# Attention of 512 queries at once, and elementwise work moved from GpSimd to VectorE, in a one-layer hybrid encoder block

## The chip, the cores and the metric

One core of one Trainium2 chip runs the whole kernel in one launch. The metric is device time in microseconds, the median of several runs. The engines are TensorE (PE: matrix products, with PEld for its weight loads), VectorE (DVE), ScalarE (ACT), GpSimd (POOL) and SyncE (SP, which here issues most DMAs; ScalarE issues those of the weights).

## The reference

2048 tokens of width 1024 go through one layer with two branches. All matrix products work in float32.

```
h    = rms_norm(x, norm_gain)
proj = h @ w_in                       # 7168 columns: q,k,v,gate of A; q,k,v,gate of R; two merge gates
A: 8 heads x 64. Each chunk of 64 frames attends to its own chunk and the 8 before it;
   score = q.k / 8 + bias by clipped distance; softmax; @ v;  times silu(gate);  @ w_out_attn
R: 8 heads, key 64, value 128. Rotary, then retention with decay by |distance|, chunk-causal,
   GroupNorm per head;  times silu(gate);  @ w_out_ret
out = rms_norm(x + (sigmoid(m_a) * A + sigmoid(m_r) * R) @ w_out, final_gain)
```

For blocks of 512 queries (four tiles of 128) the keys are cut into blocks of 128. Query tile t needs the five key blocks t to t+4, counted from 512 keys before the block: its own tile and the four before it. In the sequence's first block of queries only the blocks from number 4 on exist.

## The kernel before

**Float32 by halves.** Operands of the large products are split into a high part (a ScalarE copy, rounded) and a low part (source minus high part, on VectorE or GpSimd). A product of two is then three products: high by high, high by low, low by high. The probabilities of attention are split the same way (`pth`, `ptl`), and V's high and low halves lie side by side in one weight tile `va`, so that a product with `pth` and one with `ptl` suffice.

**Stages.** The token axis is handled in two halves (s = 0 and 1). In order of TensorE: projection p0, attention and retention of half 0, projection p1, attention and retention of half 1, branch outputs ba and br (the merge), output projection out. The gate projections g0 and g1 are the filler of attention and retention. Projections and out use Strassen's seven products per chunk (`Strassen`), with sums `t1` to `t4` of the weight blocks (`sum`) and low parts (`prepare`, `make`); a job's `lo_pool` names the products whose low part GpSimd makes.

**Order.** All dense products form one stream. `step()` puts out the next dense step (three matmuls a step in most jobs); `fill(n)` puts out n of them. `later(n, fn)` defers an operation by n steps, `put(n, dst, src)` a store by n steps. So every operation has its place in an order written by hand, and each engine keeps that order. `Sometimes` keeps it only while `strict[0]` is set; for the merge it is off, and a planner orders ScalarE, VectorE and GpSimd there, until `br1`'s third chunk sets it again ahead of out.

**Attention before.** A unit is (head h, block b of 512, half un of it): 256 queries, two tiles of 128 (a = 0, 1). `soft` multiplies a query tile with the keys of its window into the PSUM region `wide`; one step later VectorE adds the bias and finds the minimum (`least`, into a `pr` tile, `mn`), after two steps ScalarE takes the exponential and its sum, after four VectorE's reciprocal and GpSimd's multiplication normalize the tile. `weighted` then takes six key blocks of 128 in three groups of two: TensorE transposes the probabilities into `tp`, ScalarE evicts `pth`, a step later VectorE `ptl`, and `PV_LAG` = 3 steps after the transposition the products with V go into `po`. Each product has 256 columns, both query tiles, and where a tile does not see a key block, VectorE sets its 128 columns to zero. After the second unit of a block ScalarE and VectorE fold `po` into `oa`, and GpSimd multiplies it by the gate.

The unit loop puts `soft` of unit m (a = 0, two steps, a = 1, one step) ahead of the three groups of unit m-1 (one step each). For the first block of the sequence `weighted` has one group for un = 0 and two for un = 1. Attention tiles come from a ring of `E_ATT` = 12 buffers and `PR_BUFS` = 4 `pr` buffers.

**Merge and out.** `finish_yr` multiplies retention's output by gate, gain (VectorE) and reciprocal deviation (GpSimd, L1248) and splits it into resident operands `R`. `ep_br` (L1290, L1291) forms gate times product on VectorE and adds branch A's part `ta` on GpSimd; SP stores it. `fill_wo` and `place_wo` form and split the sums of `w_out`. The first chunk of out (c = 0) forms its four sums and two of its low parts on GpSimd.

Of the kernel before, what the change touches and what calls it, by code (L numbers as in the profile page):

```python
# [11 lines left out]
F32 = mybir.dt.float32  # L12
# [42 lines left out]
E_PROJ = 19  # L55
E_ATT = 12
E_RET = 22
E_MRG = 23
PR_BUFS = 4
ATT_FILLS = (1.0, 1.0)  # L60
# [13 lines left out]
def hybrid_kernel(  # L74
# [261 lines left out]
    class Strassen(Chunk):  # L336
# [15 lines left out]
        def lean(self):  # L352
            return self.job.name[0] == "p"

# [18 lines left out]
        def prepare(self, n):  # L373
            self.sums(n)
            for s in SUMS_OF:
                if s[0] == PRODUCTS[n][1]:
                    self.sum(*s)
            late = pool if n in self.job.lo_pool else dve
            self.make(n, self.b[PRODUCTS[n][1]], late)
# [907 lines left out]
    def ep_br(s):  # L1287
        def epilogue(c, i, j, ps, got):
            g, ta = got
            dve.scalar_tensor_tensor(g, g, 1.0, ps, ALU.add, ALU.mult)  # L1290
            pool.tensor_tensor(g, g, ta, ALU.add)  # L1291
            put(7, mxscr[2 * s + i][2 * c + j], g)

        return epilogue
# [3 lines left out]
    def fill_wo(k):  # L1298
# [8 lines left out]

        def place(m, t, eng):
            later(1, lambda: act.copy(R[m][0][:, k, :], t))
            later(3, lambda: eng.tensor_tensor(R[m][1][:, k, :], t, r32(R[m][0][:, k, :]), ALU.subtract))  # L1310

        def sums():
            dve.tensor_tensor(s3, a[1, 0], a[0, 0], ALU.subtract)
            place(0, a[0, 0], pool)
            dve.tensor_tensor(s2, s3, a[1, 1], ALU.add)

        def rest():
            pool.tensor_tensor(s4, a[0, 1], s2, ALU.subtract)
            place(1, a[0, 1], dve)
            pool.tensor_tensor(a[1, 0], a[1, 0], a[1, 1], ALU.add)  # L1320
            place(3, a[1, 0], dve)

# [88 lines left out]
    def attention(s, sbp, ps_wide):  # L1411
# [3 lines left out]
        kts, vts, qts, bts, uts, oas, prs = {}, {}, {}, {}, {}, {}, {}  # L1415
        units = [(h, b, un) for h in range(HEADS) for b in (2 * s, 2 * s + 1) for un in range(2)]

# [56 lines left out]

        def soft(h, b, un, a):

            t = 2 * un + a
            nm = f"{h}_{b}_{t}"
# [11 lines left out]
            for part in range(2):  # L1490
                for j0, j1 in parts:
# [3 lines left out]
                    )  # L1495
            pr = sbp.tile([P, WIN], F32, tag="pr", bufs=PR_BUFS, name=f"pr_{nm}")
            mn = small.tile([P, 1], F32, tag="mn", name=f"mn_{nm}")
            rsum = small.tile([P, 1], F32, tag="rsum", name=f"rsum_{nm}")
            bt = bts[h]

            def least():
                dve.tensor_tensor_reduce(
                    pr[:, 0:w], sp, bt[:, WIN - w:WIN], 1.0, 3.0e38, ALU.add, ALU.min, mn,
                )

            def exps():
                act.activation(pr[:, 0:w], pr[:, 0:w], AF.Exp, bias=mn, scale=-1.0, accum_out=rsum)

            def normed():
                dve.reciprocal(rsum, rsum)  # L1510
                pool.tensor_scalar(pr[:, 0:w], pr[:, 0:w], rsum, 1.0, ALU.mult, ALU.mult)
# [3 lines left out]
            later(4, normed)  # L1515
            return pr

        def weighted(h, b, un, pr2):

            nk = 6 if b > 0 else 2 * un + 2  # L1520
            lo = [0, 1] if b > 0 else [0, 0]
            hi = [nk - 1, nk]
            o = po[:, un * 256:(un + 1) * 256]
            for gr in range(nk // 2):
                js = [2 * gr + 1, 2 * gr] if gr in (0, nk // 2 - 1) else [2 * gr, 2 * gr + 1]
                tp = ACC(f"tp_{h}_{b}_{un}_{gr}")
                ok, none, parts = [], [], []
                for n, j in enumerate(js):
                    for a in range(2):
                        c = (2 * n + a) * P  # L1530
                        if lo[a] <= j < hi[a]:
                            pe.transpose(
                                tp[:, c:c + P], pr2[a][:, (j - lo[a]) * P:(j - lo[a] + 1) * P], ident
                            )
                            ok.append(c)
                        else:
                            none.append(c)
                c0, c1 = ok[0], ok[-1] + P
                assert c1 - c0 == len(ok) * P

                def part(which, gr=gr, tp=tp, none=none, parts=parts, c0=c0, c1=c1):
                    t = E(f"pt{which}_{h}_{b}_{un}_{gr}", F32R)
                    parts.append(t)
                    for c in none:
                        dve.memset(r32(t[:, c:c + P]), 0.0)
                    if which == "h":
                        act.copy(t[:, c0:c1], tp[:, c0:c1])
                    else:
                        dve.tensor_tensor(t[:, c0:c1], tp[:, c0:c1], r32(parts[0][:, c0:c1]), ALU.subtract)

                def product(gr=gr, js=js, parts=parts):
                    for n, j in enumerate(js):
                        k = 2 * un + j if b > 0 else j + 4
                        v4 = vts[h, b - 1 + k // 4][:, k % 4, :]
                        for i, t in enumerate(parts):
                            pe.matmul(
                                o, v4, t[:, 256 * n:256 * n + 256],
                                start=(gr == 0 and n == 0 and i == 0),
                                stop=(gr == nk // 2 - 1 and n == 1 and i == 1),
                            )  # L1560
                    if gr == nk // 2 - 1:
                        later(1, out_)

                part("h")
                later(1, lambda part=part: part("l"))
                later(PV_LAG, product)
                yield

            def out_():
                if un == 0:  # L1570
                    return
                oa, u = E(f"oa_{h}_{b}")[0:64], uts[h, b]
# [3 lines left out]
                put(6, oascr[h // 2][b][64 * (h % 2):64 * (h % 2) + 64], oa)  # L1576

        load_bias(0)
        load_k(0, 2 * s)
        load_q(0, 2 * s, 0)  # L1580
        fill(12)
        turn_bias(0)
        fill(6)
        for m in range(len(units) + 1):
            if m < len(units):
                h, b, un = units[m]
                if m + 1 < len(units):
                    h2, b2, un2 = units[m + 1]
                    load_q(h2, b2, un2)
                if un == 0 and m + 2 < len(units):  # L1590
                    load_k(*units[m + 2][0:2])
                if un:
                    load_u(h, b)
                if (b, un) == (2 * s, 0) and h + 1 < HEADS:
                    load_bias(h + 1)
                if (b, un) == (2 * s + 1, 0) and h + 1 < HEADS:
                    turn_bias(h + 1)
                prs[m] = [soft(h, b, un, 0)]
                fill(2 * ATT_FILL)
                prs[m].append(soft(h, b, un, 1))  # L1600
                fill(ATT_FILL)
            if m:
                for _ in weighted(*units[m - 1], prs.pop(m - 1)):
                    fill(ATT_FILL)
            if m < len(units) and un == 0:
                later(PV_LAG - 1, lambda h=h, b=b: load_vs(h, b))
        fill(PV_LAG + 9)

# [431 lines left out]
```

## Time and profile before

| | us |
|---|---|
| median of 3 runs (1924.24 to 1926.1) | 1926.05 |
| the profiled execution | 1926.96 |
| its span, first to last instruction | 1925.2 |
| PE busy | 1879.2 |
| DVE busy | 1355.6 |
| ACT busy | 930.3 |
| POOL busy | 771.7 |

In the profiled execution attention takes 345 to 560 us (half 0) and 1060 to 1321 us (half 1) of the span, ba starts at 1491, br at 1583, out at 1758. In a row `out<-in xcount | busy, mean ns | idle`, the first names are program tiles without their numbers, the busy time counts overlapping matmuls once, and the last part is what the engine waited for just before. L143 is the line of a helper that records nearly every operation, so tiles, not lines, tell operations apart there.

### The profile page before, as it was taken

How to read it: one execution, taken by the hardware profiler on the slowest of the kernel's cores; microseconds unless marked ns; L12 is line 12 of the kernel's file. 1: busy time of each engine (PE TensorE's matmuls, PEld its weight loads, DVE VectorE, ACT ScalarE, POOL GpSimd, SP SyncE). 2: the span in 40 equal slices, each digit the busy share in tenths (PEclk: the TensorE clock that was granted, in tenths of full speed). 3: DMA queues.
4: the chain of work that ended last, by engine and by line, in shares of the span. 5: the costliest groups of instructions: out<-in, count | busy, mean ns of one | idle time of the engine just before them, and what ended most of it. 6: DMA issues, size and time to landing. Idle time of an engine off the chain costs nothing. (4 is left out here: it accounts for less than half of the span.)

```text
span 1925.2 us, 31831 instructions
## 1 busy us (share of the span) xinstructions
PE 1879.2 (98%) x10437; PEld 1617.7 (84%) x10437; DVE 1355.6 (70%) x2602; ACT 930.3 (48%) x1931; POOL 771.7 (40%) x661
## 2 busy tenths in 40 slices
PE   7999999999999999999999999999999999999998
PEld 6899889888888878899889888888888878887886
DVE  6879888677756558879797777765555654557665
ACT  7555553666655445443333656664455321223554
POOL 0102105545546562002105444544564114547775
PEclk9999999999999999999999999999999999999999
DMA  6586876665559987675666555555998999987673
GB/s 197 160 282 195 274 259 218 184 186 178 174 155 281 273 241 268 224 249 180 224 237 216 156 165 175 161 157 162 271 290 263 326 356 328 319 264 234 209 234 133
DMA packets 325555, 435.91 MB, mean 226 GB/s; under 512 B 29880, under 2 KB 191184, under 8 KB 325392
## 3 DMA queue, kind: packets, MB, share of 16 engines
q1 hardware_dynamic: 260096, 368.35, 59.9%
q10 hardware_dynamic: 65296, 65.55, 11.1%
q8 instruction: 83, 1.36, 0.3%
q14 instruction: 80, 0.66, 0.1%
HBM read 288.14 MB, written 145.64 MB: 225 GB/s over the span
## 5 line engine op out<-in xcount | busy, mean ns | idle before, releaser
L143 POOL TENSOR_SCALAR pr<-pr,rsum 128x640 f32<-128x640 f32 (+4 forms) x128 | 96.0, 750 | 213.3 <-DVE ptl L143 103.4
L143 PE MATMUL ps_g_x<-r,wh_g 128*128 128x512 f32 x448 | 143.9, 402 | 1.0 <-ACT u_g L143 0.8
L143 PE MATMUL ps_g_z<-r,wh_g 128*128 128x512 f32 x448 | 143.6, 402 | 0.7 <-DVE c_g L143 0.7
L143 DVE CUSTOM_DVE_ANT_0 pr<-wide,bt 128x640 f32<-128x640 f32 (+4 forms) x128 | 94.3, 736 | 62.5 <-PE wide L143 56.2
L143 ACT ACTIVATE pr<-pr,mn 128x640 f32<-128x640 f32 (+4 forms) x128 | 98.0, 766 | 81.1 <-DVE mn L143 81.1
L143 POOL TENSOR_TENSOR l_vr<-vrt,h_vr 128x512 fp32r<-128x512 f32 x32 | 47.7, 1492 | 202.3 <-DMA qrs<-l_q 131.5
L143 DVE TENSOR_TENSOR ptl<-tp,pth 128x384 fp32r<-128x384 f32 x168 | 96.0, 572 | 41.8 <-ACT pth L143 37.6
L143 ACT CAST pth<-tp 128x384 fp32r<-128x384 f32 x168 | 84.6, 515 | 69.0 <-PE tp L143 65.3
L143 POOL TENSOR_TENSOR sl<-sm,sh 128x384 fp32r<-128x384 f32 x64 | 69.9, 1092 | 70.2 <-ACT sh L143 44.7
L143 DVE TENSOR_TENSOR sm<-sr,dm 128x384 f32<-128x384 f32 x64 | 35.6, 556 | 83.6 <-PE sr L143 31.5
L143 PEld LDWEIGHTS tp<-ident,pr 128*128 128x128 f32 x560 | 71.2, 140 | 27.4 <-POOL pr L143 2.8
L143 PE MATMUL po<-pth,va 128*128 128x256 f32 x336 | 92.4, 295 | 0.9 <-DMA va<-vas 0.9
L143 ACT CAST wh_p<-raw_p 128x512 fp32r<-128x512 f32 x111 | 68.0, 619 | 50.3 <-PE ps_p_y L143 17.9
L143 PE MATMUL tp<-ident,pr 128*128 128x128 f32 x560 | 89.1, 272 | 3.0 <-POOL pr L143 1.9
L143 PE MATMUL wide<-ka,qa 128*128 128x384 f32 (+1 forms) x448 | 88.2, 313 | 2.2 <-DVE mn L143 2.1
L143 POOL TENSOR_TENSOR wl_g<-t_g,wh_g 128x512 fp32r<-128x512 f32 x56 | 74.8, 1336 | 38.4 <-ACT wh_g L143 31.0
L143 PEld LDWEIGHTS wide<-ka,qa 128*128 128x128 f32 x448 | 74.5, 188 | 18.6 <-DVE mn L143 8.7
L143 PE MATMUL po<-ptl,va 128*128 128x256 f32 x336 | 88.3, 284 | 1.4 <-DVE ptl L143 0.2
L143 PE MATMUL ps_g_x<-r,wl_g 128*128 128x512 f32 x224 | 88.5, 395 | 0.0
L143 POOL TENSOR_TENSOR yr<-yr,rb 128x512 f32<-128x512 f32 x8 | 11.7, 1467 | 191.1 <-DVE yr L143 100.1
L143 PE MATMUL ps_g_z<-r,wl_g 128*128 128x512 f32 x224 | 88.1, 393 | 0.0
L143 POOL TENSOR_TENSOR t_g<-raw_g,t_g 128x512 f32<-128x512 f32 x56 | 73.8, 1318 | 28.7 <-DVE wl_g L143 10.6
(929 smaller groups left out, 6193.3 us busy)
## 6 DMA issues: line engine op xcount, KB each, us to landing
raw_g<-in_w_in_dram ACTq DMA_DIRECT2D x56, 512.0 KB, 5.0
raw_p<-in_w_in_dram ACTq DMA_DIRECT2D x50, 512.0 KB, 6.3
qa<-qas SPq DMA_DIRECT2D x128, 128.0 KB, 3.3
qr<-qrs SPq DMA_DIRECT2D x128, 128.0 KB, 4.9
vr<-vrs SPq DMA_DIRECT2D x64, 256.0 KB, 5.8
ka<-kas SPq DMA_DIRECT2D x56, 256.0 KB, 3.7
va<-vas SPq DMA_DIRECT2D x40, 256.0 KB, 3.5
kds<-kdt_k SPq DMA_DIRECT2D x32, 256.0 KB, 5.5
```

The costliest lines, as they stand in the source:

```text
L143: return tc.keep_in_program_order(op(*a, **k))
```

## The change

Attention handles a whole block of 512 queries as a unit (h, b). `soft` takes one query tile t = 0 to 3, `weighted` one group of key blocks: (0, 1), (2), (3), (4), (5), (7, 6); the first block of the sequence uses the last three groups. Each product has only the columns of the query tiles that see the key block. `plan` gives a unit's length in slots of one dense step, which group stands in which slot and which query tile of the next unit stands in which; `slot` puts them out, with the loads. In the first block the four query tiles share two `pr` buffers. `E_ATT` goes from 12 to 11, `PR_BUFS` from 4 to 5, and the first group of a unit is multiplied after 4 steps, not 3.

Besides, these operations go from GpSimd to VectorE: the four sums and two low parts of out's first chunk, the multiplication by the reciprocal deviation in the merge (`m` given), the sum in `ep_br`, and sums and low parts in `fill_wo` and `place_wo`.

```diff
-E_ATT = 12
+E_ATT = 11
-PR_BUFS = 4
+PR_BUFS = 5
...
         def lean(self):
-            return self.job.name[0] == "p"
+            return self.job.name[0] == "p" or self.job.name == "out" and self.c == 0
...
-            late = pool if n in self.job.lo_pool else dve
+            late = pool if n in self.job.lo_pool and not self.lean() else dve
...
-        later(lead + 2, lambda: pool.tensor_tensor(a, a, r, ALU.mult))
+        later(lead + 2, lambda: (pool if m is None else dve).tensor_tensor(a, a, r, ALU.mult))
...
-            pool.tensor_tensor(g, g, ta, ALU.add)
+            dve.tensor_tensor(g, g, ta, ALU.add)
...
-            place(0, a[0, 0], pool)
+            place(0, a[0, 0])
...
-            pool.tensor_tensor(s4, a[0, 1], s2, ALU.subtract)
+            dve.tensor_tensor(s4, a[0, 1], s2, ALU.subtract)
...
-            pool.tensor_tensor(a[1, 0], a[1, 0], a[1, 1], ALU.add)
+            dve.tensor_tensor(a[1, 0], a[1, 0], a[1, 1], ALU.add)
...
-                eng = pool if k == 2 else dve
-                eng.tensor_tensor(R[m][1][:, k, :], wo[m, k], r32(R[m][0][:, k, :]), ALU.subtract)
+                dve.tensor_tensor(R[m][1][:, k, :], wo[m, k], r32(R[m][0][:, k, :]), ALU.subtract)
...
-        def soft(h, b, un, a):
-            t = 2 * un + a
+        def soft(h, b, t):
+            un, a = divmod(t, 2)
...
             def least():
+                pair, at = (t, 0) if b > 0 else ((0, 0), (1, 0), (1, 2 * P), (0, P))[t]
+                if (h, b, pair) not in wholes:
+                    wholes[h, b, pair] = sbp.tile([P, WIN], F32, tag="pr", bufs=PR_BUFS, name=f"pr_{nm}")
+                prs[h, b, t] = wholes[h, b, pair][:, at:at + w]
...
+        def weighted(h, b, gr):
+            k0 = 0 if b > 0 else 4
+            js = ((0, 1), (2,), (3,), (4,), (5,), (7, 6))[gr]
+            tp = ACC(f"tp_{h}_{b}_{gr}")
+            c, cut, parts = 0, [], []
+            for j in js:
+                ts = range(max(0, j - 4), min(4, j + 1))
+                cut.append((j, c, ts))
+                for t in ts:
+                    at = (j - max(t, k0)) * P
+                    pe.transpose(tp[:, c:c + P], prs[h, b, t][:, at:at + P], ident)
+                    c += P
...
+            def product():
+                for j, at, ts in cut:
+                    n = len(ts) * P
+                    v4 = vts[h, b - 1 + j // 4][:, j % 4, :]
+                    for i, p in enumerate(parts):
+                        pe.matmul(
+                            po[:, ts[0] * P:ts[0] * P + n], v4, p[:, at:at + n],
+                            start=j == (0 if b > 0 else 4) and i == 0, stop=gr == 5 and j == 6 and i == 1,
+                            skip_group_check=True,
+                        )
+                if gr == 5:
+                    later(1, out_)
...
+            part("h")
+            later(1, lambda: part("l"))
+            later(PV_LAG + (gr == 0), product)
+
+        def plan(b):
+            if b == 0:
+                return 9, {2: 3, 4: 4, 6: 5}, {1: 0, 3: 1, 5: 2, 7: 3}
+            return 12, {0: 0, 2: 1, 4: 2, 6: 3, 8: 4, 10: 5}, {2: 0, 6: 1, 8: 2, 10: 3} if s else {2: 0, 4: 3, 6: 1, 8: 2}
+
+        def slot(m, n, groups, softs):
+            after = units[m + 1] if m + 1 < len(units) else None
+            if n == 0 and after:
+                h, b = after
+                load_q(h, b, 1)
...
+            if n == 6:
+                if m + 2 < len(units):
+                    load_k(*units[m + 2])
+                if m >= 0:
+                    load_u(*units[m])
+            if n in groups and m >= 0:
+                weighted(*units[m], groups[n])
+            if n in softs and after:
+                soft(*after, softs[n])
...
-        fill(6)
-        for m in range(len(units) + 1):
...
-        fill(PV_LAG + 9)
+        fill(2)
+        for m in range(-1, len(units)):
+            length, *plans = plan(units[m][1] if m >= 0 else 2 * s + 1)
+            for n in range(length):
+                slot(m, n, *plans)
+                if n == length - 2 and m + 2 < len(units):
+                    load_q(*units[m + 2], 0)
+                if n == length - 1 and m + 1 < len(units):
+                    load_vs(*units[m + 1])
+                fill(ATT_FILL if m >= 0 or n > 1 else 0)
+        fill(PV_LAG + 3)
```

More of the change, by code (lines that the diff above doesn't have):

```diff
@@ L1306, in fill_wo, with place @@
         wo[4, k], wo[5, k], wo[2, k], wo[6, k] = s2, s3, a[1, 1], s4
-        def place(m, t, eng):
+        def place(m, t):
             later(1, lambda: act.copy(R[m][0][:, k, :], t))
-            later(3, lambda: eng.tensor_tensor(R[m][1][:, k, :], t, r32(R[m][0][:, k, :]), ALU.subtract))
+            later(3, lambda: dve.tensor_tensor(R[m][1][:, k, :], t, r32(R[m][0][:, k, :]), ALU.subtract))
         def sums():
             dve.tensor_tensor(s3, a[1, 0], a[0, 0], ALU.subtract)
-            place(0, a[0, 0], pool)
+            place(0, a[0, 0])
             dve.tensor_tensor(s2, s3, a[1, 1], ALU.add)
         def rest():
-            pool.tensor_tensor(s4, a[0, 1], s2, ALU.subtract)
-            place(1, a[0, 1], dve)
-            pool.tensor_tensor(a[1, 0], a[1, 0], a[1, 1], ALU.add)
-            place(3, a[1, 0], dve)
+            dve.tensor_tensor(s4, a[0, 1], s2, ALU.subtract)
+            place(1, a[0, 1])
+            dve.tensor_tensor(a[1, 0], a[1, 0], a[1, 1], ALU.add)
+            place(3, a[1, 0])
         later(10, sums)
@@ L1415, in attention @@
         kts, vts, qts, bts, uts, oas, prs = {}, {}, {}, {}, {}, {}, {}
-        units = [(h, b, un) for h in range(HEADS) for b in (2 * s, 2 * s + 1) for un in range(2)]
+        units = [(h, b) for h in range(HEADS) for b in (2 * s, 2 * s + 1)]
+        wholes = {}
         def load_k(h, b):
@@ L1495, in soft @@
                     )
-            pr = sbp.tile([P, WIN], F32, tag="pr", bufs=PR_BUFS, name=f"pr_{nm}")
             mn = small.tile([P, 1], F32, tag="mn", name=f"mn_{nm}")
@@ L1501, in least @@
             def least():
+                pair, at = (t, 0) if b > 0 else ((0, 0), (1, 0), (1, 2 * P), (0, P))[t]
+                if (h, b, pair) not in wholes:
+                    wholes[h, b, pair] = sbp.tile([P, WIN], F32, tag="pr", bufs=PR_BUFS, name=f"pr_{nm}")
+                prs[h, b, t] = wholes[h, b, pair][:, at:at + w]
                 dve.tensor_tensor_reduce(
-                    pr[:, 0:w], sp, bt[:, WIN - w:WIN], 1.0, 3.0e38, ALU.add, ALU.min, mn,
+                    prs[h, b, t], sp, bt[:, WIN - w:WIN], 1.0, 3.0e38, ALU.add, ALU.min, mn,
                 )
             def exps():
+                pr = prs[h, b, t]
                 act.activation(pr[:, 0:w], pr[:, 0:w], AF.Exp, bias=mn, scale=-1.0, accum_out=rsum)
             def normed():
+                pr = prs[h, b, t]
                 dve.reciprocal(rsum, rsum)
@@ L1515, in soft @@
             later(4, normed)
[L1516 to L1567, printed above, removed]
@@ new lines, in weighted, with part @@
+        def weighted(h, b, gr):
[10 more added lines that the diff above has]
+                    c += P
+            def part(which):
+                p = E(f"pt{which}_{h}_{b}_{gr}", F32R)
+                parts.append(p)
+                if which == "h":
+                    act.copy(p[:, 0:c], tp[:, 0:c])
+                else:
+                    dve.tensor_tensor(p[:, 0:c], tp[:, 0:c], r32(parts[0][:, 0:c]), ALU.subtract)
+            def product():
[10 more added lines that the diff above has]
+                    later(1, out_)
@@ L1569, in out_ @@
             def out_():
-                if un == 0:
-                    return
                 oa, u = E(f"oa_{h}_{b}")[0:64], uts[h, b]
@@ L1576, in out_ @@
                 put(6, oascr[h // 2][b][64 * (h % 2):64 * (h % 2) + 64], oa)
+            part("h")
[10 more added lines that the diff above has]
+                load_q(h, b, 1)
+                if b == 2 * s and h + 1 < HEADS:
+                    load_bias(h + 1)
+                if b == 2 * s + 1 and h + 1 < HEADS:
+                    turn_bias(h + 1)
+            if n == 6:
[7 more added lines that the diff above has]
+                soft(*after, softs[n])
@@ L1578, in attention @@
         load_bias(0)
-        load_k(0, 2 * s)
-        load_q(0, 2 * s, 0)
+        load_k(*units[0])
+        load_q(*units[0], 0)
         fill(12)
         turn_bias(0)
-        fill(6)
-        for m in range(len(units) + 1):
[L1585 to L1606, printed above, removed]
```

## The prediction

> **What bounds the kernel now.** I read the page's totals first, then busy time by stage, then TensorE's groups with shapes kept apart, its instructions in order of time, and its waits.
>
> The page's head and the row of PE:
>
> ```profile
> span 1925.2 us, 31831 instructions
> PE 1879.2 (98%) x10437; PEld 1617.7 (84%) x10437; DVE 1355.6 (70%) x2602; ACT 930.3 (48%) x1931; POOL 771.7 (40%) x661
> ```
>
> TensorE is busy 98% of the span, so the time follows what it is given to do plus its few waits. The two attention stages, by stretches (length, then busy time of PE, PEld, DVE, ACT and POOL, clock, DMA share, GB/s):
>
> ```profile
> 345.00:560.00 215.00, 211.91 (x1233) 180.12 (x1232) 157.08 (x456) 135.14 (x316) 117.40 (x132) 1.00 0.58 173
> 1060.00:1321.00 261.00, 256.58 (x1540) 221.91 (x1539) 189.26 (x520) 157.61 (x343) 126.44 (x128) 1.00 0.53 159
> ```
>
> PE idles 3.1 us in the first and 4.4 us in the second, at full clock; no other engine is over 73%. A busy PE hides cost, since matmuls overlap: a matmul's price is the distance from its start to the next start. PE in order of time (start, duration, operation, shape, count):
>
> ```profile
> 420.16 0.40 PE L143 MATMUL ps_g_v<-r,wl_g 128*128 128x512 f32 x1
> 420.39 0.33 PE L143 MATMUL wide<-ka,qa 128*128 128x128 f32 x2
> 420.56 0.33 PE L143 MATMUL po<-pth,va 128*128 128x256 f32 x1
> ...
> 421.78 0.28 PE L143 MATMUL po<-pth,va 128*128 128x256 f32 x1
> ...
> 422.25 0.63 PE L143 MATMUL ps_g_v<-r,wh_g 128*128 128x512 f32 x2
> ...
> 427.55 0.51 PE L143 MATMUL wide<-ka,qa 128*128 128x384 f32 x2
> 427.90 0.28 PE L143 MATMUL po<-pth,va 128*128 128x256 f32 x1
> ```
>
> The prices: 512 columns 0.23 us (420.16 to 420.39); two of 128 columns together 0.17, so 0.085 each; 256 columns 0.1175 (four `po` from 421.78 to 422.25); 384 columns 0.175 (two from 427.55 to 427.90).
>
> **The change, part 1: the products with V.** The groups before:
>
> ```profile
> L143 PE MATMUL po<-pth,va 128*128 128x256 f32 x336 | 92.4, 295 | 0.9 <-DMA va<-vas 0.9
> L143 PE MATMUL po<-ptl,va 128*128 128x256 f32 x336 | 88.3, 284 | 1.4 <-DVE ptl L143 0.2
> ```
>
> 672 products of 256 columns, 672 x 0.1175 = 79.0 us. After it each key block of 128 multiplies only the query blocks that see it. A full block of 512 queries (24 of them: 8 heads x 3) has key blocks that serve 1, 2, 3, 4, 4, 3, 2, 1 query tiles; each is multiplied twice (high and low part), which is 4 products each of 128, 256, 384 and 512 columns. A first block (8 heads) has only its own four key blocks, serving 4, 3, 2, 1: 2 of each width. Together 24 x 4 + 8 x 2 = 112 of each width: 112 x (0.085 + 0.1175 + 0.175 + 0.23) = 68.0 us. The saving is 11.0 us, all on PE, nothing beside it.
>
> The transposes stay 560, in 168 groups of three or four, so the evictions into `pth` and `ptl` stay; the score matmuls stay 448. The memsets of missing blocks go from VectorE. The dense steps interleaved are the same: 18 + 96 + 72 + 12 = 198 in the first attention stage before, 24 + 168 + 6 = 198 after; 222 and 222 in the second. So the work beside attention does not move.
>
> TensorE's waits in the two attention stretches, and who of PEld waited for the transposes' parts:
>
> ```profile
> PE tp L143 <- POOL pr L143: 0.9, 2, 0.8
> PE po L143 <- DMA va<-vas: 0.9, 1, 0.9
> PE wide L143 <- DVE mn L143: 0.8, 1, 0.8
> ```
>
> ```profile
> PE wide L143 <- DVE mn L143: 1.3, 1, 1.3
> PE tp L143 <- DVE ptl L143: 1.1, 2, 0.6
> PE tp L143 <- POOL pr L143: 1.0, 1, 1.0
> ```
>
> ```profile
>   PEld po L143: 4.2, 14
> ```
>
> **Late low parts.** 14 times the weight load of a `po` product waited for `ptl`, 4.2 us in all. They fall on a unit's first group. VectorE is in order there: in the rows below `oa` runs at 1133.64 and ends at 1134.30, and the next unit's first `po` product starts at 1134.43, its low part still behind `oa` on VectorE. After the change a unit's first group is multiplied one step later (lag 4, not 3), and its memsets are gone. I take -3.0, between 0 and -4.2. Next late is the `po` bank itself, below.
>
> **The softmax chain gets a step less.** One tile's way, with the reuse of `po`, in order of time over all engines:
>
> ```profile
> 1127.84 0.74 PE L143 MATMUL wide<-ka,qa 128*128 128x384 f32 x4
> ...
> 1128.62 0.82 DVE L143 CUSTOM_DVE_ANT_0 pr<-wide,bt 128x640 f32<-128x640 f32 x1 [0.22 <-PE wide L143]
> ...
> 1133.57 0.15 DVE L143 RECIPROCAL rsum<-rsum 128x1 f32<-128x1 f32 x1
> 1133.64 0.66 DVE L143 TENSOR_TENSOR oa<-po,oa 64x512 f32<-64x512 f32 x1
> ...
> 1133.89 0.80 POOL L143 TENSOR_SCALAR pr<-pr,rsum 128x640 f32<-128x640 f32 x1 [3.80 <-DVE rsum L143]
> ...
> 1134.43 0.36 PE L143 MATMUL po<-pth,va 128*128 128x256 f32 x1
> ```
>
> From the scores at 1127.84 to the normalized tile at 1134.69 it is 6.85 us. Before, the second tile of a unit has 7 steps until its first transposition, 7 x 261/222 = 8.2 us in the second stage. After, query tiles 1, 2 and 3 have 6: tile 2 goes from slot 8 to slot 2 of the next unit, tile 3 from 10 to 4. 6 steps at that mean are 7.1 us: 0.2 us of slack. VectorE's and GpSimd's own operations in it are only 0.82 + 0.15 + 0.80 = 1.8 us, most of the rest is queueing, so it can shrink; but GpSimd's sums for the gates stand in front of some. 64 uses (two a unit) are exposed. Bounds: 0, and 64 x 0.80 = 51 us if each waited for one more GpSimd operation of that size. Three waits of this kind cost 1.9 us at the old slack; I take +2.5, near the old rows, because slots that carry tiles are longer than the mean.
>
> **The output bank.** From a block's last product to the next block's first are four steps, and the read-out `oa` ends 0.13 us ahead of the latter (1134.30 and 1134.43). In the second stage the change leaves three steps, but VectorE's read is then queued ahead of the next tile's minimum instead of behind one. 0 to 15 blocks x 0.6 us = 9; I take +1.
>
> SP issues Q's parts 4 to 8 slots ahead, the ring of attention buffers shrinks from 12 to 11, and the one DMA wait is 0.9 us; zero, with the DMA wait in PE's list as its sign. The two `wide` waits at the stages' starts I leave as they are (the second half of Q is asked for two steps earlier or later).
>
> **Part 2: from GpSimd to VectorE.** GpSimd's largest group in the merge (29 under this line, three more under another), then, from the start of the output projection, VectorE alone and beside GpSimd, TensorE's long wait, and the stretch around it:
>
> ```profile
> L1291 POOL TENSOR_TENSOR gr<-gr,ta 128x512 f32<-128x512 f32 x29 | 44.5, 1540 | 56.9 <-DVE gr L1290 33.5 <-issue 16.1 <-DMA yr<-ors 3.3
> ```
>
> ```profile
> 1765.07 0.68 DVE L143 TENSOR_TENSOR wl_out<-raw_out,wh_out 128x512 fp32r<-128x512 f32 x1
> 1765.67 1.75 DVE L143 TENSOR_TENSOR r<-wo,r 128x512 fp32r<-128x512 f32 x1
> ```
>
> ```profile
> 1766.53 0.73 PE L143 MATMUL ps_out_x<-r,wh_out 128*128 128x512 f32 x2 [2.73 <-ACT u_out L143]
> ```
>
> ```profile
> 1754.00:1780.00 26.00, 22.93 (x92) 17.77 (x90) 24.61 (x21) 11.38 (x22) 23.71 (x15) 0.93 0.75 252
> ```
>
> Moved are 32 adds of the merge, 24 multiplications of `yr`, 12 of `fill_wo`, 4 of `place_wo`, and 6 of the first output chunk: 78, at 0.68 us 53 us for VectorE instead of 1.54 us each on GpSimd. They lie beside a full PE everywhere except at 1754 to 1780, where VectorE (24.6 of 26 us) and GpSimd (23.7) are both full and slow each other: 1.75 us against 0.68 for the same shape. There PE waits 2.73 us and then runs at clock 0.93, 0.07 x 26 = 1.8 us more. After: 21 + 13 operations at 0.68 = 23.1 us of VectorE, so it stays full, but each link is shorter. SP's stores of the merged rows wait for VectorE, done sooner, and no queue is passed. ScalarE, which makes `u_out`, also waited for a DMA, which stays. Bounds: -4.5 (both go) and +4.5 (a second such wait, should VectorE's longer queue hold ScalarE). I take -2.5.
>
> By the Trainium skill, TensorE: Matmul & The Clock Gate, section "What's actually happening", the array drops to half clock after an idle window of about 3.4 us. The row shows the clock at 0.93 behind an idle of 2.73 us, so the measurement decides. By the page this stall would have no clock price, and the term would be 1.8 us smaller: 1914.9 instead of the sum below.
>
> **Sum**: -11.0 - 3.0 + 2.5 + 1.0 - 2.5 = -13.0 us. The profiled execution took 1926.96 us (span 1925.2), 0.9 over the median of 1926.05; 1926.96 - 13.0 = 1913.96, and against the median 1913.1.
>
> **Rivals.**
> - *Narrow products pay a full weight load.* Each product loads its weights anew, and in retention, with three of 128 columns in a row, the later ones are 0.11 us apart:
>
> ```profile
> 604.33 0.28 PE L143 MATMUL o<-sl,vr 128*128 128x128 f32 x1
> 604.44 0.27 PE L143 MATMUL o<-sh,vr 128*128 128x128 f32 x1
> ```
>
> Then 112 x 0.025 = 2.8 us are lost: 1915.9. Against it: the pairs here follow a wide matmul, as at 420.39. The Trainium skill, same page, section "LDWEIGHTS (loading the stationary operand)", gives columns / 1.2 ns, an estimate of 107 ns for 128; by that rule the saving would be 8.5 us. The 0.17 us pair speaks against the rule for the first of two.
> - *The bank's reuse eats half*: 15 blocks x 0.6 us = 9 instead of 1: 1921.1. For it: `oa` ends 0.13 us before the next product now. Against: what delays it, the minimum in front, is behind it after.
> - *All stalls go*: -11.0 - 4.2 - 4.5 and no new waits: 1906.4, or lower with the starts.
> - *No change to measure*: the exposed tiles wait 0.24 us each (64 x 0.24 = 15.5, the other terms' -15.5): 1926.
> - *Slower*: transposes starve. At 0.24 us a use it turns; at 0.5 us it is 32 us against 15.5, 1942. For it: 0.2 us of slack and GpSimd 55% busy in the first stage. Against: 1.9 us of such waits now, and most of the 6.85 us is pacing by the steps.
>
> **How the numbers follow.** What a measurement can tell here is about 0.2%, 3.9 us. Forecast 0.53, narrow products 0.16, bank 0.12, all stalls gone 0.07, no change 0.05, slower 0.07. The first four are faster: 0.88; same 0.05; slower 0.07. The range 1906 to 1922 reaches over the first three (0.81) and leaves out 0.19.
>
> **What would show it.** `po` by shape: 224 each for `pth` and `ptl`, 112 each of 128, 256, 384 and 512 columns in all, and the two attention stretches about 5 us shorter each. "PEld po" behind `ptl` near 1 us. Waits of `tp` for `pr` under 5 us; over 15 I am wrong. DVE's operations of the merge near 0.7 us, and the 2.73 us wait shorter, the clock there 1.00. A wait of `po` for `oa`, or of `wide` for DMA `qa`, over 3 us would be the bank or the SP queue.

## The result and the profile after

| us | before | after |
|---|---|---|
| median of 5 runs each, on one chip | 1924.24 | 1909.69 |
| lowest to highest | 1921.62 to 1926.1 | 1905.84 to 1913.15 |
| the profiled execution | 1926.96 | 1909.69 |

The ratio is 0.9927, interval 0.9907 to 0.9946: 14.55 us faster. Forecast were 1913.1, in a range of 1906 to 1922, and a drop of 12.95. The two profiled executions are 17.3 us apart, since the one of before lies 2.7 us over its median here; terms read from the traces add up to that figure. The interval of the ratio leaves room for a drop of 10.4 to 17.9 us.

The head of the changed kernel's page, and its row of engines:

```profile
span 1907.9 us, 31062 instructions
...
PE 1866.9 (98%) x10213; PEld 1604.4 (84%) x10213; DVE 1355.7 (71%) x2456; ACT 933.1 (49%) x1931; POOL 665.3 (35%) x583
```

TensorE is as full as before in a shorter span: work went from the engine that bounds the kernel. GpSimd lost 106 us of busy time. VectorE's stayed, though 78 operations came: with the memsets gone it has 146 instructions fewer. The stretches that answer to those shown of before (the two attention stages, then 4 us ahead of out's first matmul to 22 us behind it; columns: length, busy PE, PEld, DVE, ACT, POOL, clock, DMA share, GB/s):

```profile
341.00:558.00 217.00, 213.68 (x1162) 180.01 (x1161) 150.90 (x362) 139.38 (x324) 120.11 (x135) 1.00 0.58 172
1052.00:1313.00 261.00, 258.39 (x1445) 220.25 (x1444) 179.11 (x395) 160.78 (x352) 134.55 (x134) 1.00 0.54 162
```

```profile
1742.50:1768.50 26.00, 26.00 (x116) 21.56 (x115) 25.78 (x38) 11.78 (x24) 12.56 (x7) 1.00 0.71 237
```

Before, the third had PE at 22.93 of 26 and the clock at 0.93; now PE has no gap and the full clock, though VectorE is fuller than ever (25.78). GpSimd is at 12.56 us there, against 23.71 before. The products with V by shape, `pth` only:

```profile
L143 PE MATMUL po<-pth,va 128*128 128x512 f32 x56 | 23.1, 412 | 0.0
...
L143 PE MATMUL po<-pth,va 128*128 128x384 f32 x56 | 21.7, 387 | 0.0
...
L143 PE MATMUL po<-pth,va 128*128 128x256 f32 x56 | 18.6, 333 | 0.0
...
L143 PE MATMUL po<-pth,va 128*128 128x128 f32 x56 | 14.8, 264 | 2.2 <-DVE oa L143 2.1
```

56 of each, 112 with `ptl`, as counted. The last row holds the new wait: the narrow product is the first of its block, and waits until VectorE has read the bank.

To see where time went I cut each trace at fixed marks. Attention 0 goes from the first gate matmul to the first retention matmul, attention 1 from the last matmul of projection p1 to its first retention matmul, br from its first matmul to out's first, out from its first start to its last. Between such marks, in us:

```
              attention 0  attention 1    br      out
before            256.77      303.92    174.77   158.34
after             253.15      296.34    174.08   152.35
att_alone         253.12      296.36    175.64   158.32
moves_all         256.26      303.98    174.08   152.35
moves_out0        256.14      303.97    176.25   156.59
moves_merge       256.17      303.95    174.08   153.03
late_store        255.84      304.01    184.79   157.98
swap              252.07      296.32    174.08   152.35
widened           253.48      296.27    174.08   152.35
lag5              255.18      293.24    174.08   152.35
gr_last           256.78      304.02    174.39   157.47
yr_only           256.11      303.99    174.09   158.24
gr_all            256.12      303.95    174.08   153.84
best              253.24      292.86    174.08   152.35
```

Attention gave 3.6 + 7.6 = 11.2 us, out 6.0, all other stages together 0.1. Kernels that share a stage's code agree there within 0.1 us in attention 1 and 0.9 in attention 0; totals scatter by 0.2%. So the verdicts below on parts of a stage are read from this table.

### The profile page after: what moved, and what is told of

Its sections match the earlier page's. It is cut to its first block, busy times and chain, and to the rows that moved or that the text cites. A ratio compares the mean times of both kernels' runs of the same rounds, so it can differ in the third digit from the quotient of the medians.

```text
span 1907.9 us, 31062 instructions
## 1 busy us (share of the span) xinstructions
PE 1866.9 (98%) x10213; PEld 1604.4 (84%) x10213; DVE 1355.7 (71%) x2456; ACT 933.1 (49%) x1931; POOL 665.3 (35%) x583
## 3 DMA queue, kind: packets, MB, share of 16 engines
q10 hardware_dynamic: 65296, 65.55, 11.2%
## 5 line engine op out<-in xcount | busy, mean ns | idle before, releaser
L143 POOL TENSOR_SCALAR pr<-pr,rsum 128x640 f32<-128x640 f32 (+4 forms) x128 | 100.0, 781 | 197.7 <-DVE rsum L143 130.7
L143 DVE TENSOR_TENSOR ptl<-tp,pth 128x512 fp32r<-128x512 f32 (+1 forms) x168 | 100.3, 597 | 91.7 <-ACT pth L143 77.8
L143 POOL TENSOR_TENSOR t_out<-raw_out 128x512 f32<-128x512 f32 x7 | 14.1, 2008 | 263.2 <-DVE wl_out L143 263.2
L143 ACT CAST pth<-tp 128x512 fp32r<-128x512 f32 (+1 forms) x168 | 85.3, 507 | 38.9 <-PE tp L143 34.2
L143 PE MATMUL wide<-ka,qa 128*128 128x384 f32 (+1 forms) x448 | 94.9, 327 | 2.9 <-DVE mn L143 2.7
L143 PEld LDWEIGHTS ps_g_x<-r,wh_g 128*128 128x128 f32 x448 | 79.6, 189 | 13.9 <-ACT u_g L143 2.3
L143 PEld LDWEIGHTS ps_g_z<-r,wh_g 128*128 128x128 f32 x448 | 79.5, 188 | 12.4
L143 DVE TENSOR_TENSOR wl_p<-raw_p,wh_p 128x512 fp32r<-128x512 f32 x111 | 79.5, 723 | 7.7 <-ACT wh_p L143 5.4
```

The source lines that it names most:

```text
L143: return tc.keep_in_program_order(op(*a, **k))
```

## The experiments

### Do the two parts add?

`att_alone` is the changed kernel with all 78 operations back on GpSimd; `moves_all` is the kernel before with only those 78 on VectorE.

```
att_alone:  lean, late, finish_yr, ep_br, fill_wo, place_wo  as before
moves_all:  the same six places  as after; attention as before
```

> The attention part of the change alone; the 78 operations stay on GpSimd. Theory (two parts that add): the stretch from the first gate product to retention shrinks by 3.6 us in half 0 and from the last projection product to retention by 7.6 us in half 1, as in the changed kernel, and the 2.73 us wait of TensorE for u_out at the start of the output projection stays, with its cold clock; 11 us less, about 1914 us. Rival (the start of the output projection depends on how the whole lines up, not on who does the adds): that wait is gone here too, and the time is 17 us less, about 1908 us.

Measured: 1912.26 us, ratio 0.9951 (0.9931 to 0.9971).

> Only the 78 operations moved from GpSimd to VectorE, attention as before. Theory: the output projection from its first to its last matmul takes 152.4 us instead of 158.3, the branch outputs keep 92 and 175 us; 6 us less, about 1919 us. Rival (alignment): the wait at the start of the output projection stays in part, 0 to 2 us less.

Measured: 1912.59 us, ratio 0.9955 (0.9938 to 0.9973). In the table the first has the changed kernel's attention (11.2 us shorter) and before's out, the second the reverse (out 6.0 us shorter): together the 17.2 of the change. The parts add in the table; the ratios allow it, but their intervals are too wide to show it alone. TensorE's waits in `att_alone` keep the old one of out (3.1 us) beside the new one of the bank:

```profile
PE ps_out_x L143 <- ACT u_out L143: 3.1, 1, 3.1
...
PE po L143 <- DVE oa L143: 2.2, 7, 0.4
```

### What does a product of 128 columns cost?

Two theories: 0.085 us, as the prediction took it, or some 0.11, set by its weight load. In a unit's first and last group the pair of 128 columns comes ahead of a pair of 256. `swap` puts it behind, so that a dense matmul follows it; `widened` makes every product of 128 columns 256 wide (the added columns get terms that don't belong to them).

```diff
-            js = ((0, 1), (2,), (3,), (4,), (5,), (7, 6))[gr]
+            js = ((1, 0), (2,), (3,), (4,), (5,), (6, 7))[gr]      # swap
...
-                            start=j == (0 if b > 0 else 4) and i == 0, stop=gr == 5 and j == 6 and i == 1,
+                            start=j == (1 if b > 0 else 4) and i == 0, stop=gr == 5 and j == 7 and i == 1,
```
```diff
-                    n = len(ts) * P
+                    n = max(len(ts), 2) * P                        # widened
+                    f = ts[0] if j else 0
+                    f = 2 if j == 7 else f
...
-                            po[:, ts[0] * P:ts[0] * P + n], v4, p[:, at:at + n],
+                            po[:, f * P:f * P + n], v4, p[:, at:at + n],
```

> The changed kernel with the products of 128 columns behind those of 256 in the groups (0, 1) and (7, 6), which become (1, 0) and (6, 7). Theory (each product loads its weights and cannot follow closer than that load, 0.11 us, so a product of 128 columns costs 0.11 wherever it stands): attention takes the same, 253.1 us in half 0 and 296.3 us in half 1 between the marks used before, within 0.5. Rival (the price is the distance to the next start, 0.06 and 0.11 for a pair of 128 columns, and 0.17 for the product of 256 behind it, 0.05 too much, which another order avoids): 56 groups x 0.0525 us less, 1.3 us in half 0 and 1.7 us in half 1.

Measured: 1906.06 us, ratio 0.9927 (0.9901 to 0.9953); attention -1.08 and -0.02 us.

> The changed kernel with the 112 products of 128 columns made 256 wide, over the neighbouring 128 columns, which adds wrong terms to those columns of the output. Theory (a product of 128 costs a weight load, 0.11 us, one of 256 costs 0.1175): 0.4 us more in half 0 and 0.5 us more in half 1. Rival (0.085 us for one of 128, as the prediction had it): 1.6 us and 2.1 us more.

Measured: 1906.25 us, ratio 0.9925 (0.9897 to 0.9953); attention +0.33 and -0.07 us. At 0.085 the 112 wider products had to cost 3.7 us; at 0.11 under 1. They cost 0.3, and attention 1, where the scatter is 0.1 us, shows none of the 2.1 us that 0.085 asked of it: a product of 128 columns is as dear here as one of 256. TensorE's order shows how. First the changed kernel, a unit's first group between two dense steps (start, duration):

```profile
439.21 0.40 PE L143 MATMUL ps_g_x<-r,wl_g 128*128 128x512 f32 x1
439.45 0.22 PE L143 MATMUL po<-pth,va 128*128 128x128 f32 x1
439.51 0.27 PE L143 MATMUL po<-ptl,va 128*128 128x128 f32 x1
439.62 0.33 PE L143 MATMUL po<-pth,va 128*128 128x256 f32 x1
439.79 0.28 PE L143 MATMUL po<-ptl,va 128*128 128x256 f32 x1
439.91 0.63 PE L143 MATMUL ps_g_x<-r,wh_g 128*128 128x512 f32 x2
440.38 0.40 PE L143 MATMUL ps_g_x<-r,wl_g 128*128 128x512 f32 x1
```

Then the same place in `widened`, and in `swap`:

```profile
440.25 0.28 PE L143 MATMUL po<-pth,va 128*128 128x256 f32 x1
...
440.73 0.62 PE L143 MATMUL ps_g_x<-r,wh_g 128*128 128x512 f32 x2
441.19 0.40 PE L143 MATMUL ps_g_x<-r,wl_g 128*128 128x512 f32 x1
```

```profile
439.65 0.28 PE L143 MATMUL po<-pth,va 128*128 128x256 f32 x1
439.76 0.28 PE L143 MATMUL po<-ptl,va 128*128 128x256 f32 x1
439.88 0.22 PE L143 MATMUL po<-pth,va 128*128 128x128 f32 x1
439.94 0.28 PE L143 MATMUL po<-ptl,va 128*128 128x128 f32 x1
440.05 0.67 PE L143 MATMUL ps_g_x<-r,wh_g 128*128 128x512 f32 x2
440.56 0.39 PE L143 MATMUL ps_g_x<-r,wl_g 128*128 128x512 f32 x1
```

After: the pair of 128 takes 0.06 and 0.11 between starts, 0.17 as forecast. But the first 256 behind it then takes 0.17 (439.62 to 439.79) in place of 0.1175. The weight loads (PEld) of the second, third and fourth product set the pace, since they start 0.11 us apart:

```profile
439.45 0.19 PEld L143 LDWEIGHTS po<-ptl,va 128*128 128x128 f32 x1
439.56 0.19 PEld L143 LDWEIGHTS po<-pth,va 128*128 128x128 f32 x1
439.67 0.19 PEld L143 LDWEIGHTS po<-ptl,va 128*128 128x128 f32 x1
```

The narrow product starts its successor early, and the one behind that has to wait for its weights: the debt shows one start later. The four together take 0.46, 0.11 each for the narrow ones and 0.12 for the wide. In `swap` the debt lands on the dense pair behind (0.51 for two in place of 0.47). From the first product to the end of the two dense ones it is 0.93 in the changed kernel, 0.94 in `widened`, 0.91 in `swap`. Why `swap` gained 1.1 us in half 0 alone isn't settled: a gain from the order itself would stand in half 1 too, and attention 0 scatters by up to 0.9 in the kernels with the attention of before.

### Does the output bank hold a block's start?

VectorE's and TensorE's way through one change of block, after (the rows of other operations left out):

```profile
1125.26 0.28 PE L143 MATMUL po<-ptl,va 128*128 128x256 f32 x1
...
1127.34 0.58 ACT L143 COPY oa<-po 64x512 f32<-64x512 f32 x1
...
1127.96 0.68 DVE L143 TENSOR_TENSOR oa<-po,oa 64x512 f32<-64x512 f32 x1 [0.99 <-ACT oa L143]
...
1128.70 0.33 PE L143 MATMUL po<-pth,va 128*128 128x128 f32 x1 [0.15 <-DVE oa L143]
```

ScalarE folds the bank 1.8 us after the last product has ended, for its queue is full until then; then VectorE reads it, and TensorE stands. `lag5` multiplies a unit's first group a step later still; `best` does so in half 1 only, and in half 0 also brings the first unit's query tiles in the order 0, 1, 2, 3.

```diff
-            later(PV_LAG + (gr == 0), product)
+            later(PV_LAG + 2 * (gr == 0), product)          # lag5
+            later(PV_LAG + (1 + s) * (gr == 0), product)    # best
...
+            if m < 0 and not s:                             # best
+                plans[1] = {2: 0, 4: 1, 6: 2, 8: 3}
```

> The changed kernel with the first group of a unit multiplied 5 steps behind its transposition instead of 4. Theory (in half 1 the first product waits 0.15 to 0.6 us for the read-out oa of the block before, in 8 of 16 units, 3.5 us together): these waits go, half 1 takes 3 to 3.5 us less between its marks (about 293), half 0 at most 0.5 less; 1906 us. Rival (the step longer holds two more buffers of 11 and SyncE's loads of Q and V wait for them): new waits of the scores or products for DMA, no gain or up to 3 us more.

Measured: 1904.21 us, ratio 0.9924 (0.9903 to 0.9945). Attention 1 is 3.1 us shorter, attention 0 2.0 us longer, where the theory had at most 0.5 less. Of the rival's new waits for loads there is one of 0.3 us, for Q. Over both halves TensorE's waits for the minimum grew from 2.7 us in four to 3.5 in five; the rest of the 2.0 is open:

```profile
PE wide L143 <- DVE mn L143: 3.5, 5, 1.1
```

> The changed kernel with the first group's lag of 5 steps in half 1 only, and at the very start of half 0 the query tiles in the order 0, 1, 2, 3 instead of 0, 3, 1, 2, so that the second part of Q is needed two slots later. Expected: half 1 between its marks 293.2 us as with lag 5, half 0 253.1 us less up to 1.2 of the wait of 1.28 us at its start, 4 us less in all than the changed kernel, 1905 us. Rival (what half 1 gains is lost again in retention's waits for its loads): no difference to the changed kernel.

Measured: 1903.93 us (1899.6 to 1906.85), ratio 0.9922 (0.9903 to 0.9942). Attention 1 is 3.5 us shorter than in the changed kernel, attention 0 as there: the new order of tiles gave nothing. All of TensorE's waits in its second attention stage, with no `po` behind `oa` any more:

```profile
PE tp L143 <- POOL pr L143: 0.9, 2, 0.7
PE wide L143 <- DVE mn L143: 0.5, 1, 0.5
```

The bank cost 3.5 us. The changed kernel's own trace says the same: in half 1, 17 groups start with a narrow product right behind a dense one, and in 8 of them the way from the one start to the next is 0.38 to 0.83 us instead of 0.24, 3.4 us more together. By medians `best` can't be told from the change (0.9922 and 0.9927, on different chips); in the traces its four stages of the table add up to the least.

### What held the start of out?

Six kernels, each the one before with a part of the moves: the sums of out's first chunk and its low parts (`moves_out0`); the 32 adds of `ep_br` and the 24 multiplications of `finish_yr` (`moves_merge`); the multiplications alone (`yr_only`); the adds alone (`gr_all`); the last four adds alone (`gr_last`); and no move, but the merged rows' stores six steps later (`late_store`).

```diff
+            return self.job.name[0] == "p" or self.job.name == "out" and self.c == 0    # moves_out0
...
+            late = pool if n in self.job.lo_pool and not self.lean() else dve     # moves_out0
...
+        later(lead + 2, lambda: (pool if m is None else dve).tensor_tensor(a, a, r, ALU.mult))    # moves_merge, yr_only
...
+            dve.tensor_tensor(g, g, ta, ALU.add)                                  # moves_merge, gr_all
+            (dve if s and c == 3 else pool).tensor_tensor(g, g, ta, ALU.add)      # gr_last
...
-            put(7, mxscr[2 * s + i][2 * c + j], g)
+            put(13, mxscr[2 * s + i][2 * c + j], g)                               # late_store
```

> Only the four sums and two low parts of the first output chunk go to VectorE. Theory (they stand in the in-order chain that holds ScalarE, and with it u_out): the 2.73 us wait shrinks below 1 us, the clock stays at 1.00 around it, 4 to 6 us less. Rival (VectorE is slowed by GpSimd's other adds, those of the weight sums and of the merge, which still run beside it at 1.7 us an operation): the wait stays above 2 us, less than 2 us gained.

Measured: 1920.34 us, ratio 0.9994 (0.9982 to 1.0005). Out is 1.8 us shorter, br 1.5 longer. That the chunk's own sums were the cause has fallen; the wait is still there, and one in br's last chunk has grown from 0.4 us:

```profile
PE ps_out_x L143 <- ACT u_out L143: 2.2, 1, 2.2
...
PE ps_br_(0, 0)_20577 L143 <- DVE wl_br_(0, 1)_20526 L300: 1.5, 1, 1.5
```

What out gained is about the price of the clock: behind this wait it stays at 1.00, where before it fell (0.69 in 5.5 us, below). In `yr_only`, with a shorter wait of 1.9 us, it falls again. So a wait near 2 us may or may not cost the clock besides. The 5.5 us behind the wait, in `moves_out0` and in `yr_only`, the clock third from the end:

```profile
1762.30:1767.80 5.50, 5.02 (x21) 3.83 (x22) 5.50 (x5) 2.56 (x5) 4.87 (x3) 1.00 0.88 304
```

```profile
1757.00:1762.50 5.50, 5.48 (x16) 4.06 (x17) 5.50 (x4) 2.56 (x5) 5.50 (x4) 0.69 0.90 332
```

> Only the 32 adds of gated branches and the 24 multiplications by the reciprocal deviation go to VectorE. Theory: the branch outputs lie beside a full TensorE, so they keep 92 and 175 us, and the start of the output projection keeps most of its wait, since GpSimd still makes the sums there: 0 to 1.5 us less. Rival (stores and loads queued behind these adds on SyncE set the start of the output projection): the wait of 2.73 us goes, 4 to 6 us less.

Measured: 1917.11 us, ratio 0.9976 (0.9962 to 0.9989). Out is 5.3 of the 6.0 us shorter, and the wait gone. The rival had the outcome: the merge's operations held out's start. That they did so by SyncE's queue, as it says, this run does not show.

> The kernel before with one edit: the store of a merged row is put out 13 steps behind its product instead of 7; every add stays on GpSimd. Theory (SyncE's queue: the loads of x for the output projection stand behind stores that wait for GpSimd's adds, and ScalarE's load of the next weights waits for such a load): the output projection, 158.3 us from its first to its last matmul, falls below 155, and TensorE's wait for u_out below 1 us. Rival (GpSimd's adds hold its sums and slow VectorE to 1.7 us an operation, which the edit leaves as it is): it stays between 156.5 and 158.5 us with a wait of 2 us or more.

Measured: 1931.13 us, ratio 1.0061 (1.0043 to 1.0079). Out stays at 157.98. The 10 us are lost within br: 4.9 in one wait 70 us behind its start, 2.8 behind that wait, where the clock is 0.50 over 5.5 us, and 1.9 in three more waits. The first of them, and the wait of out:

```profile
PE ps_br_(0, 0)_19861 L143 <- ACT wh_br_(0, 0)_19784 L299: 4.9, 1, 4.9
...
PE ps_out_x L143 <- ACT u_out L143: 2.1, 1, 2.1
```

> The kernel before with only the four adds of gated branches in the last chunk of br1 on VectorE; 28 adds and 24 multiplications stay on GpSimd. Theory (the adds right ahead of the output projection hold up loads and sums there): the output projection, 158.3 us between first and last matmul, falls below 154.5. Rival (it takes the whole merge off GpSimd: the delay builds up over the stage): it stays above 156.5.

Measured: 1922.42 us, ratio 1.0019 (1.0 to 1.0038); out 157.47. ScalarE's wait for the load of x is gone, and another, longer one stands there, for a sum on GpSimd (4.76 us against 3.86). That theory has fallen too.

> The kernel before with only the 24 multiplications by the reciprocal deviation on VectorE. Theory (the adds ahead of the output projection are the cause, these end earlier): the output projection stays at 158 us, within 1. Rival (GpSimd's backlog from these reaches the output projection): below 156 us.

Measured: 1918.76 us, ratio 1.0002 (0.9988 to 1.0015); out 158.24. TensorE's wait is 0.8 us shorter, but the stage is not: the multiplications alone gain nothing.

> The kernel before with all 32 adds of gated branches on VectorE; the 24 multiplications stay on GpSimd. Theory (GpSimd's delay builds up over these adds; the last four alone were too few and the multiplications had no part): the output projection, 158.3 us between its first and last matmul, falls to 153 to 154 us, as with the whole merge moved, and TensorE's wait for u_out below 0.5 us. Rival (it takes both groups off): 156 us or more.

Measured: 1915.17 us, ratio 0.9976 (0.9964 to 0.9987); out 153.84, 4.5 of the 6.0. All the adds together hold the start; the last four are not enough. How the delay spreads over the other 28 no run tells.

The place where the delay ends is the same throughout. ScalarE casts the high parts of out's first products in a fixed order, and the copy `u_out`, which TensorE needs 5.4 us after out's first matmul, stands behind the third of these casts. Starts against out's first matmul, what the third cast waited for just before, when SyncE issued the first load of x for out, and the length of out:

```
              2nd cast  3rd cast  waited for        u_out  x issued    out
before          -1.99      4.06   load of x, 3.86    7.70     -0.91   158.34
att_alone       -1.96      4.42   load of x, 4.20    8.07     -0.90   158.32
late_store      -3.99      4.18   load of x, 5.99    7.83     -1.59   157.98
yr_only         -2.04      3.24   load of x, 3.10    6.89     -1.02   158.24
gr_last         -2.88      4.07   GpSimd sum, 4.76   7.72     -1.82   157.47
moves_out0      -2.03      3.83   load of x, 3.67    7.47     -0.99   156.59
gr_all          -6.76      0.34   TensorE, 4.92      3.99     -5.62   153.84
moves_merge     -6.75     -0.99   load of x, 3.58    2.92     -6.60   153.03
moves_all       -6.75     -1.48   VectorE sum, 3.10  2.92     -8.87   152.35
after           -6.76     -1.46   VectorE sum, 3.12  2.92     -8.87   152.35
```

Wherever the third cast is late, the copy comes 3.65 us behind it. Two of those rows, before and after, as the traces have them:

```profile
1762.26 0.62 ACT L143 CAST wh_out<-raw_out 128x512 fp32r<-128x512 f32 x1 [3.86 <-DMA xr<-in_x_dram]
```

```profile
1745.09 0.62 ACT L143 CAST wh_out<-raw_out 128x512 fp32r<-128x512 f32 x1 [3.12 <-DVE t_out L143]
...
1749.47 0.59 ACT L143 COPY u_out<-ps_out_x 128x512 f32<-128x512 f32 x1 [0.63 <-PE ps_out_x L143]
```

The length of the wait in front of the cast says little: `moves_merge` waits 3.58 us for the load of x and loses nothing at `u_out`, since it waits 5 us earlier. What counts is that the second cast comes 6.75 us ahead of out in the four kernels without GpSimd's adds, and 2 to 4 in the six with some. Shown is the place, and that all 32 adds together move it.

The column of x narrows the link. SyncE issues its first load of x 0.9 to 1.8 us ahead of out's first matmul in the six kernels with adds on GpSimd, and 5.6 to 8.9 us ahead in the four without. So the delay is already in SyncE's queue when the loads of x go out, where they stand behind the stores of the merged rows. What holds that queue stays open: `late_store` was meant to test it, moved the issue by only 0.7 us and disturbed br instead. SP's waits for the sums in the merge, before, and then after:

```profile
SPq L143 <- POOL gr L1291: 41.6, 17, 5.6
```

```profile
SPq L143 <- DVE gr L1291: 24.6, 14, 4.1
```

With the adds that stand under another line, within br, it is 42.3 us before and 29.5 after.

## Why the prediction was right, point by point

The time, the sign and the range were right. The sum of -13.0 came out in the traces as -11.2 in attention and -6.0 in out, 17.2 in all; the medians give 14.55. The terms were off in both directions. The measured ones are read from prices and waits in the traces; only the two stage sums were measured as a whole:

| term | forecast | measured |
|---|---|---|
| products with V | -11.0 | -7.7 |
| late low parts | -3.0 | -2.7 |
| softmax chain a step shorter | +2.5 | about -3 |
| output bank | +1.0 | +3.5 |
| other waits in attention | 0 | -0.2 |
| merge and start of out | -2.5 | -6.0 |

- **Products.** The step that failed is the price of 128 columns, "two of 128 columns together 0.17, so 0.085 each". At the prices between starts 112 x (0.11 + 0.12 + 0.175 + 0.232) = 71.3 us, 7.7 under 79.0. The first of the rivals was right with its 0.11. The Trainium skill, TensorE: Matmul & The Clock Gate, section "LDWEIGHTS (loading the stationary operand)", gives columns / 1.2 ns, an estimate of 107 ns for 128; the trace agrees, with weight loads 0.11 us apart. The prediction set its own row above that rule, and its row had been read one start short: in the rows it quotes, the 256 behind the pair starts at 420.56 and lasts 0.33, not 0.28 as the others do, and the next start, a row left out there, came 0.18 later, not 0.1175:

```profile
420.74 0.28 PE L143 MATMUL po<-ptl,va 128*128 128x256 f32 x1
```

- **Low parts.** PEld's waits for `ptl`, 4.2 us in 14, are 1.0 + 0.5 us in 5:

```profile
PEld po L143 <- DVE ptl L143: 1.0, 3, 0.4
```

```profile
PEld po L143 <- DVE ptl L143: 0.5, 2, 0.3
```

  The step held, as far as a weight load's wait is TensorE's: TensorE's own waits for `ptl` were 0.2 us and are 0.5. The first two rows together can be read directly. From start to next start between the marks, all products with V took 89.1 us and take 79.0: 10.1 less, beside the 10.4 of the two rows.
- **Softmax chain.** TensorE's waits in the two attention stages, 341 to 558 us and 1052 to 1313 us, have no row of `tp` behind `pr` or `ptl` any more:

```profile
PE wide L143 <- DVE mn L143: 2.3, 3, 1.1
PE po L143 <- DVE ptl L143: 0.5, 2, 0.3
```

```profile
PE po L143 <- DVE oa L143: 2.1, 7, 0.4
PE wide L143 <- DVE mn L143: 0.5, 1, 0.5
```

  Before there were 0.9, 1.1 and 1.0 us; the 1.1 are waits for `ptl`, which are not of this chain. The sign was wrong: the forecast made the 0.2 us of slack the point and added 2.5. It had read that slack from one tile, whose way from the start of its minimum to its normalized end is 6.07 us; the mean of the second stage was 5.34 and is 4.70 (4.67 and 4.60 in the first). Its own remark, that most of the 6.85 us is pacing by the steps and can shrink, was the better guide.
- **Bank.** The term was mis-sized, though within its bounds of 0 to 9. It argued from VectorE's queue; what came first was ScalarE's fold, ahead of VectorE's read, as the rows at 1127.34 and 1127.96 show. The sign named for it, `po` behind `oa` in TensorE's waits, is there with 2.1 us, and the late starts of blocks and `best` put it at 3.4 to 3.5.
- **Other waits.** The load of V (0.9 us) is gone, the waits of `wide` grew from 2.1 to 2.8. The five rows of attention add up to -10.1; of the 11.2, 1.1 us is left unassigned.
- **Merge and out.** GpSimd's work did hold the start, and the clock fell behind the wait. But the prediction looked for it where VectorE and GpSimd slow each other, at 1754 to 1780, and had the merge's operations "beside a full PE everywhere" else, with "no queue is passed". That step failed: the sums of that place alone left a wait of 2.2 us, and the adds of the merge gave 4.5 of the 6.0, with SyncE's queue late behind them. The size, -6.0, is past the bound of -4.5. The wait itself is 2.7 us. The clock behind it cost (1 - 0.69) x 5.5 = 1.7:

```profile
1766.50:1772.00 5.50, 5.47 (x17) 4.35 (x18) 5.50 (x4) 2.58 (x5) 5.50 (x5) 0.69 0.81 301
```

  A second wait of out, 0.7 us for `c_out`, isn't in the forecast at all and is gone as well; 0.9 is spread. The step "ScalarE also waited for a DMA, which stays" failed: the load of x was issued late as long as GpSimd had the adds, and in the changed kernel no wait for it is left ahead of `u_out`. The rule of the Trainium skill weighed in the prediction, by which this stall had no clock price, was not borne out: the clock fell behind a wait of 2.7 us, and is 1.00 with that wait gone. That it stayed at 1.00 behind the 2.2 us of `moves_out0` shows that the price is not sure either.

So the good total owes much to luck: it expected 3.3 us too much of the products and 2.5 too little cost of the bank, against 5.5 too little gain of the transpositions' waits and 3.5 of out. The two attention stages, forecast about 5 us shorter each, are 3.6 and 7.6 shorter.

## What to carry to other kernels

Read the price of a short matmul over the next two starts, not one: a narrow product that outruns the next weight load leaves its debt there, and cutting from 256 columns to 128 saved nothing here. At the start of a stage look for the one queue in which everything stands in order (here ScalarE's casts), and ask when each entry becomes ready, not how long it waits: small operations of an engine that is 40% busy over the whole span moved that by 5 us. A wait of TensorE can also cost clock behind it, here 1.7 us or nothing for waits of about 2 us, so separate the two when comparing. And cut traces at fixed marks: attention 1 agreed to 0.1 us between kernels with the same code, where totals of one kernel scattered by 4 and more.

## What had not been expected of the hardware

With its operations gone, GpSimd is idle for 263 us, and its first one then takes 4.03 us, where VectorE goes on beside it at its lone pace. GpSimd's row, and VectorE's in the same time:

```profile
1753.94 4.03 POOL L143 TENSOR_TENSOR t_out<-raw_out 128x512 f32<-128x512 f32 x1 [263.18 <-DVE wl_out L143]
```

```profile
1755.53 0.69 DVE L143 TENSOR_TENSOR wl_out<-t_out,wh_out 128x512 fp32r<-128x512 f32 x1
1756.13 0.68 DVE L143 TENSOR_TENSOR r<-ws,r 128x512 fp32r<-128x512 f32 x1
```

Before, both were slowed in turn, 1.75 us for VectorE and 1.74 for GpSimd against 0.68 and 1.29 alone. The Trainium skill, SBUF — State Buffer, section "SBUF: two separate sides", gives a shared port to whichever of the two starts first, for its whole instruction, and blocks the other. The rows of before agree with that in kind: both take longer, though less than the sum of 0.68 and 1.29. In the row of 4.03 us only GpSimd was held back. A span of GpSimd is rough, and no run here tells the idle time from the port as its cause.
